# Softmax over a pair of PSUM banks: one maximum and one exponential for 1024 keys in the second block's attention

## The chip, the cores and the metric

The kernel runs on one core of a Trainium2 chip. The metric is the device time of one execution in microseconds (us). Three runs of the kernel before gave 3281.88, 3284.83 and 3296.58 us; the median, 3284.83 us, is what the change is measured against.

A core has five engines with a queue each, which run in the order in which the program was written down for them: TensorE (PE in the profile; PEld are its weight loads), VectorE (DVE), ScalarE (ACT), GpSimd (POOL) and SyncE (SP, which issues the transfers here). Matrix products go to PSUM, which has eight banks of 512 float32 per partition. DVE and ACT read them there.

## The reference

Two transformer blocks over 1024 tokens of width 1024. The second one runs two mixers side by side on the same normalized input, a grouped-query attention and a gated delta rule in both directions, and mixes their outputs. What the change touches is the attention:

```python
def gqa_attention(q, k, v):
    ...
    def block(qi):
        ...
        pr = jax.nn.softmax(s, axis=-1).astype(v.dtype)
```

There are 8 heads of 128 channels and 2 key heads; the scores of one query run over all 1024 keys, are scaled by 1/sqrt(128), and their softmax weighs the values. All of it is in float32.

## The kernel before

A product that must be as exact as float32 is split: `split` (L285 to L292) makes of an operand a rounded high part on ACT (L288, or on DVE) and the remainder on DVE or POOL (L292), and `mm3` (L278) adds three products, high by high, high by low and low by high, at L281, L282 and L283. So each product of 512 columns is three matmuls.

PSUM is handed out by hand. Eight tiles of one bank each are made once, and at the start of each stage `banks` says which banks serve which kind of tile (a tag), in turn. A tag may have a list of banks that it takes once, ahead of the ones that it takes in turn; by it a stage can start in banks that the stage before has already left. The tables stand at the head of the file (`B_DELTA`, `B_ATT2`).

Two stages of the second block matter here. The delta rule runs head by head. `delta_front` prepares a head's chunks. `delta_back` (from L1530) then walks through the 8 chunks of 128 tokens in both directions side by side, with a state from chunk to chunk: for each chunk and direction the products L1560 and L1562, a multiplication on DVE (L1568), the product L1576, the new state on DVE (L1583), and the output's products L1590 and L1591 with two more operations on DVE. In front of it and once within it, `correct` (L1540) makes products at L1547 and a copy at L1549. Behind the chunks stands the output's norm (L1606 to L1615), which needs ACT, DVE and POOL in turn. In `B_DELTA` the tag `wt` is that of `correct`, `vs` that of the chunk products and `o` that of the output's.

`attention2` (L1618) follows the last head. It transposes the keys (L1633, four transposes to a bank) and splits them and the values, and then runs 64 tiles of 128 queries: the queries in two halves, 8 heads in each, 4 tiles in each head, so 16 units of 4 tiles. `scores` makes a tile's 128 by 1024 scores in two banks, three matmuls in each, takes a maximum of each half on DVE as soon as that half stands (L1668), joins them and scales (L1670), and runs an exponential with a running sum for each half on ACT (L1672). DVE adds the two sums and inverts (L1674, L1675), and POOL multiplies the row (L1676). On the first tile of a unit the unit's queries are loaded, transposed (L1654) and split. `values` transposes a finished row by 128 keys (L1687), four to a bank of tag `tr`, splits each four, and after a unit's fourth tile runs the 24 matmuls with the values into the bank of tag `pv`, and DVE multiplies by the gate (L1697). `scores` is written five tiles ahead of `values`. Once in the loop stands the load and split of the weights `w_br_att_2` that the next stage needs (L1707, L307, L288 and L292).

The order on each queue is not that of the text. A scheduler takes the whole program, with its data dependencies and the tiles' reuse, and lays each engine's instructions down by the order of writing and by when it expects them to be ready. So the attention's start is interleaved with the last head of the delta rule where banks and memory allow it, and a change of banks can move instructions on all queues.

## Time and profile before

| What | us |
|---|---|
| Median of three runs (3281.88 to 3296.58) | 3284.83 |
| The profiled execution: span from its first to its last instruction | 3279.6 |
| PE busy in that span | 2982.4 (91%) |
| DVE busy | 2276.4 (69%) |
| ACT busy | 1422.1 (43%) |
| POOL busy | 1338.1 (41%) |

The page gives the profiled execution by its span; its own time isn't listed, and the median of the runs is 5.2 us above the span. A busy share is a mean over a long program with many stages. Where the change is made is a stretch of some 280 us, and what is read there is which engine is idle, and what ended its idle time. The durations of matmuls overlap: the distance between two starts tells what one costs PE.

### The profile page before, as it was taken

The page shows a single profiled execution, that of the slowest core. Times are in us where ns is not written, and L with a number is a line of the kernel's source. Part 1 is how long each engine was busy: PE and PEld are TensorE (multiplying, and loading weights), DVE is VectorE, ACT ScalarE, POOL GpSimd, SP SyncE. Part 2 cuts the span into 40 slices and gives each one's busy share as a digit, 9 for nine tenths or more (in the row PEclk, how much of TensorE's full clock was granted, in tenths as well). Part 3 has the DMA queues.
Part 4 walks back from the last instruction along what each step waited for, and adds up shares of the span by engine and source line. Part 5 has one row for each costly group of instructions (what it writes and reads, how often), then busy time and mean ns, then how long its engine had stood idle before and what let it go on. Part 6 is the DMA issues. An engine that isn't in the chain of part 4 may idle for free.

```text
span 3279.6 us, 47090 instructions
## 1 busy us (share of the span) xinstructions
PE 2982.4 (91%) x15982; PEld 2419.7 (74%) x15982; DVE 2276.4 (69%) x5568; ACT 1422.1 (43%) x2929; POOL 1338.1 (41%) x1364
## 2 busy tenths in 40 slices
PE   6988878998988789998999999999998989999898
PEld 2866667787666567776777888888887878778776
DVE  6699977865899949687765766685677588722322
ACT  3466417712666258334233334235434376621322
POOL 3432445565324354566533334334334242333422
PEclk8998989999998899999999999999998999999999
DMA  6122253332121231333333324324333221254421
GB/s 187 42 67 69 65 174 109 99 112 72 43 91 52 73 102 52 98 97 107 96 118 94 92 89 116 102 91 122 114 97 113 56 97 49 81 183 139 169 81 65
DMA packets 280013, 317.76 MB, mean 97 GB/s; under 512 B 97600, under 2 KB 180928, under 8 KB 279772
## 3 DMA queue, kind: packets, MB, share of 16 engines
q1 hardware_dynamic: 279772, 314.75, 31.5%
q8 instruction: 126, 2.06, 0.3%
q14 instruction: 115, 0.94, 0.1%
HBM read 226.48 MB, written 88.19 MB: 96 GB/s over the span
## 4 chain that ended last, share of the span: by engine, by line
PE 33%; DVE 8%; DMA 5%; ACT 2%; issue 2%; POOL 1%; SPq 0%; POOLq 0%; ACTq 0%; DVEq 0%
PE bank L281 8%; PE bank L282 8%; PE bank L283 8%; DVE block L1461 1%; DVE mem_float L1459 1%; PE bank L1687 1%; DVE mem_float32r L292 1%; ACT mem_float32r L288 1%; DVE mem_float L1668 1%; POOL mem_float32r L292 1%; DMA mem_float<-in_w_in_dram 1%; DMA mem_float<-in_w_br_dn_dram 1%; PE bank L1560 1%; PE bank L1547 1%; PE bank L1591 1%
## 5 line engine op out<-in xcount | busy, mean ns | idle before, releaser
L281 PE MATMUL bank<-mem_float32r 128*128 128x512 f32 (+2 forms) x2500 | 1007.0, 406 | 129.1 <-ACT mem_float32r L288 53.9
L282 PE MATMUL bank<-mem_float32r 128*128 128x512 f32 (+2 forms) x2508 | 999.7, 399 | 20.3 <-POOL mem_float32r L292 19.9
L283 PE MATMUL bank<-mem_float32r 128*128 128x512 f32 (+2 forms) x2500 | 979.7, 397 | 20.2 <-DVE mem_float32r L292 11.7
L281 PEld LDWEIGHTS bank<-mem_float32r 128*128 128x128 f32 (+1 forms) x2500 | 485.4, 194 | 249.1 <-ACT mem_float32r L288 64.7
L282 PEld LDWEIGHTS bank<-mem_float32r 128*128 128x128 f32 (+1 forms) x2508 | 487.7, 194 | 119.9 <-POOL mem_float32r L292 32.0
L283 PEld LDWEIGHTS bank<-mem_float32r 128*128 128x128 f32 (+1 forms) x2500 | 483.6, 194 | 119.0 <-POOL mem_float32r L292 12.3
L292 POOL TENSOR_TENSOR mem_float32r<-mem_float,mem_float32r 128x512 fp32r<-128x512 f32 (+3 forms) x158 | 220.1, 1395 | 276.4 <-ACT mem_float32r L288 204.9
L292 DVE TENSOR_TENSOR mem_float32r<-bank,mem_float32r 128x512 fp32r<-128x512 f32 (+3 forms) x392 | 233.3, 616 | 139.2 <-ACT mem_float32r L288 137.9
L292 POOL TENSOR_TENSOR mem_float32r<-block,mem_float32r 128x512 fp32r<-128x512 f32 (+3 forms) x189 | 247.2, 1314 | 176.0 <-ACT mem_float32r L288 167.4
L288 ACT ACTIVATE mem_float32r<-bank 128x512 fp32r<-128x512 f32 (+3 forms) x392 | 199.2, 543 | 114.4 <-PE bank L1687 46.8
L288 ACT ACTIVATE mem_float32r<-mem_float 128x512 fp32r<-128x512 f32 (+4 forms) x153 | 93.5, 614 | 325.9 <-DMA mem_float<-in_w_in_dram 144.8
L740 DVE TENSOR_SCALAR_CACHE_REDUCE block<-mem_float 128x384 bf16<-128x384 int16 (+7 forms) x280 | 229.2, 819 | 6.6 <-ACT mem_float L723 3.7
L276 POOL TENSOR_TENSOR mem_float<-mem_float 128x1 f32<-128x1 f32 (+3 forms) x136 | 121.4, 898 | 213.5 <-DVE mem_float L274 183.6
L288 ACT ACTIVATE mem_float32r<-block 128x512 fp32r<-128x512 f32 (+3 forms) x199 | 114.9, 585 | 158.6 <-DMA block<-in_w_in_dram 111.7
L1676 POOL TENSOR_SCALAR mem_float<-mem_float 128x1024 f32<-128x1024 f32 x64 | 72.8, 1137 | 156.8 <-DVE mem_float L1675 133.6
L281 PE MATMUL bank<-block,mem_float32r 128*128 128x512 f32 x300 | 119.9, 400 | 6.5 <-ACT mem_float32r L288 6.5
L283 PE MATMUL bank<-block,mem_float32r 128*128 128x512 f32 x300 | 118.1, 395 | 0.0
L1459 DVE TENSOR_TENSOR mem_float<-block,block 64x31 f32<-64x31 f32 (+15 forms) x248 | 94.8, 382 | 33.1 <-DMA block<-ud 27.1
L282 PE MATMUL bank<-block,mem_float32r 128*128 128x512 f32 x292 | 115.4, 395 | 0.0
L1219 DVE SCALAR_TENSOR_TENSOR mem_float<-mem_float 128x512 f32<-128x512 f32 x128 | 108.9, 869 | 0.3
L1461 DVE TENSOR_TENSOR block<-block,mem_float 64x31 f32<-64x31 f32 (+15 forms) x248 | 98.6, 398 | 6.1
L1672 ACT ACTIVATE mem_float<-bank,mem_float 128x512 f32<-128x512 f32 x128 | 86.9, 685 | 24.0 <-DVE mem_float L1675 14.0
(530 smaller groups left out, 6159.5 us busy)
## 6 DMA issues: line engine op xcount, KB each, us to landing
block<-in_w_in_dram SPq DMA_DIRECT2D x124, 256.0 KB, 2.7
block<-in_w_ada_dram SPq DMA_DIRECT2D x42, 512.0 KB, 4.4
mem_float<-in_w_in_dram SPq DMA_DIRECT2D x60, 256.0 KB, 2.8
mem_float<-in_w_out_dram SPq DMA_DIRECT2D x32, 256.0 KB, 2.6
x<-mem_float SPq DMA_DIRECT2D x16, 512.0 KB, 2.9
mem_float<-x SPq DMA_DIRECT2D x16, 512.0 KB, 3.2
block<-row_d SPq DMA_DIRECT2D x16, 512.0 KB, 4.1
qkv_d<-mem_float SPq DMA_DIRECT2D x32, 256.0 KB, 2.4
```

What stands on the lines that cost most here:

```text
L276: nc.gpsimd.tensor_tensor(out, out, self.mhalf[:, :n], op=OP.pow)
L281: mm(ps, ah, bh, start=start, stop=False)
L282: mm(ps, ah, bl, start=False, stop=False)
L283: mm(ps, al, bh, start=False, stop=stop)
L288: nc.scalar.activation(hi, src, AF.Copy)
L292: e.tensor_tensor(lo, src, f32(hi), op=OP.subtract)
L740: nc.vector.tensor_scalar(junk[:, :n], flat(key, blocks[j]), thr[:, j:j + 1], None, op0=op, op1=OP.add, accum_out=cnt[:, j:j + 1])
L1219: nc.vector.scalar_tensor_tensor(a, raw[:, r0 + j:r0 + j + 512], cw[:, ci, j:j + 1], a, op0=OP.mult, op1=OP.add)
L1459: nc.vector.tensor_tensor(t3, un[:, 0:b, b:b + 1].to_broadcast([64, b, n]), R[:, b:b + 1, b:32].to_broadcast([64, b, n]), op=OP.mult)
L1461: nc.vector.tensor_tensor(R[:, 0:b, b:32], R[:, 0:b, b:32], t3, op=OP.subtract)
L1672: nc.scalar.activation(p[:, c * 512:c * 512 + 512], ss[c], AF.Exp, scale=S2, bias=mx[:, 2:3], accum_out=mx[:, 3 + c:4 + c])
L1676: nc.gpsimd.tensor_scalar(p, p, mx[:, 5:6], 1.0, op0=OP.mult, op1=OP.mult)
```

## The change

A pair of PSUM banks can now be one tile of 1024 columns. The lower four banks stay single. The upper four belong to a region that is given up and taken again when the attention starts, as two pairs, and once more when the last stage starts, as four single banks. A query tile's scores go to one pair. One maximum over 1024 columns takes the place of two over 512 and the joining of them, one exponential the place of two, and the addition of the two sums goes. Per query tile that is 128 to 64 maxima and 128 to 64 exponentials in all, and 64 additions fewer. The number and size of the matmuls is the same.

The banks of the delta rule and of the attention are distributed anew. The delta rule's chunk products and outputs (`vs`, `wt`, `o`), which had banks 4 to 7, have banks 0 to 3, and its other tags the upper four. The attention's transposes begin in bank 2 (the delta rule's `wt`), then take 2, 0 and 1 in turn; `pv` is bank 3. Its first five score tiles all take the lower pair (banks 4 and 5), and those behind them the two pairs in turn. Before, the first five score tiles took banks 1 and 2, and the transposes began in banks 0 and 3.

The small tile `mx` has four columns in place of six and lies elsewhere in memory. Line numbers of the changed kernel are larger by up to 10: the maximum is L1678, its scaling L1679, the exponential L1680, the inversion L1681, POOL's product L1682; the transposes of the keys are L1644, of the queries L1665 and of the rows L1693.

```diff
-B_DELTA = dict(acc=("", (0, 1)), tr=("", (2, 3)), vs=("", (4, 5)), wt=("", (6,)), o=("", (7,)))
-B_ATT2 = dict(s=([1, 2] * 5, (1, 2, 3, 4)), tr=([0, 3] * 3, (0, 5, 6)), pv=("", (7,)))
+B_DELTA = dict(acc=("", (4, 5)), tr=("", (6, 7)), vs=("", (0, 1)), wt=("", (2,)), o=("", (3,)))
+B_ATT2 = dict(s=([4] * 5, (4, 5)), tr=([2] * 3, (2, 0, 1)), pv=("", (3,)))
...
-        self.bank = [ps.tile([P, 512], F32, name=f"bank{j}") for j in range(8)]
+        self.bank = [ps.tile([P, 512], F32, name=f"bank{j}") for j in range(4)]
+        self.upper = None
+        self.upper_banks("bank", 512)
...
+    def upper_banks(self, name, n):
+
+        if self.upper:
+            self.upper.close()
+        self.upper = self.ctx.enter_context(ExitStack())
+        ps = self.upper.enter_context(self.tc.tile_pool(name=self.uid("ps"), bufs=1, space=PSUM))
+        self.bank[4:] = [ps.tile([P, n], F32, name=self.uid(name)) for _ in range(2048 // n)]
...
         self.y_d = self.dram.tile([P, 8, S], F32, name="y2_d")
+        self.upper_banks("pair", 1024)
         self.banks(**B_ATT2)
...
-                mx = ap.tile([P, 6], F32, tag="mx2", bufs=8, name=self.uid("mx2"))
-                ss = []
+                mx = ap.tile([P, 4], F32, tag="mx2", bufs=8, name=self.uid("mx2"))
+                s = self.psum("s", (P, S))
                 for c in range(2):
-                    s = self.psum("s")
                     sl = slice(c * 512, c * 512 + 512)
-                    self.mm3(s, qT[0][:, t, :], qT[1][:, t, :], kT[0][:, g, sl], kT[1][:, g, sl], True, True)
-                    nc.vector.tensor_reduce(mx[:, c:c + 1], s, axis=AX.X, op=OP.max)
-                    ss.append(s)
-                nc.vector.tensor_scalar(mx[:, 2:3], mx[:, 0:1], mx[:, 1:2], -S2, op0=OP.max, op1=OP.mult)
-                for c in range(2):
-                    nc.scalar.activation(p[:, c * 512:c * 512 + 512], ss[c], AF.Exp, scale=S2, bias=mx[:, 2:3],
-                                         accum_out=mx[:, 3 + c:4 + c])
-                nc.vector.tensor_tensor(mx[:, 5:6], mx[:, 3:4], mx[:, 4:5], op=OP.add)
-                nc.vector.reciprocal(mx[:, 5:6], mx[:, 5:6])
-                nc.gpsimd.tensor_scalar(p, p, mx[:, 5:6], 1.0, op0=OP.mult, op1=OP.mult)
+                    self.mm3(s[:, sl], qT[0][:, t, :], qT[1][:, t, :], kT[0][:, g, sl], kT[1][:, g, sl], True, True)
+                nc.vector.tensor_reduce(mx[:, 0:1], s, axis=AX.X, op=OP.max)
+                nc.vector.tensor_scalar(mx[:, 1:2], mx[:, 0:1], -S2, None, op0=OP.mult)
+                nc.scalar.activation(p, s, AF.Exp, scale=S2, bias=mx[:, 1:2], accum_out=mx[:, 2:3])
+                nc.vector.reciprocal(mx[:, 3:4], mx[:, 2:3])
+                nc.gpsimd.tensor_scalar(p, p, mx[:, 3:4], 1.0, op0=OP.mult, op1=OP.mult)
                 return p
...
         wB = self.whole_w(pb, "w_br_dn_2", "b")
+        self.upper_banks("bank", 512)
         self.banks(**B_FIN)
```

What moves is read from the order of the two programs. First PE where the attention begins. Before, with the last head's first chunk products (L1547, L1560) around them; `bank1` and `bank2` hold the first scores:

```order
L1547 MATMUL bank6_69<-mem_float32_59,block8_5_10637 128x128
L1560 MATMUL bank5_68<-block5_7_10636,block4_5_12052 128x128
L1633 MATMUL bank3_66<-mem_float32_59 128x128 x4
L281 MATMUL bank1_64<-mem_float32r_58 128x512
L282 MATMUL bank1_64<-mem_float32r_58 128x512
L281 MATMUL bank2_65<-mem_float32r_58 128x512
L282 MATMUL bank2_65<-mem_float32r_58 128x512
L1576 MATMUL bank4_67<-block8_5_10637,block7_1_94 128x128
L1591 MATMUL bank7_70<-block8_5_10637,block9_7_12098 128x128
L283 MATMUL bank1_64<-mem_float32r_58 128x512
L283 MATMUL bank2_65<-mem_float32r_58 128x512
L1576 MATMUL bank5_68<-block8_5_10637,mem_float32_59 128x128
```

In the changed kernel the first scores stand here, behind the products of the last chunk (L1570 and L1572 are the old L1560 and L1562, L1600 and L1601 the old L1590 and L1591; `pair_3271` are banks 4 and 5):

```order
L1665 MATMUL bank0_63<-mem_float32_59 128x128 x4
L1570 MATMUL bank1_64<-block5_7_10639,block4_5_12055 128x128
L1572 MATMUL bank1_64<-block7_1_97,block8_5_10640 128x128
L1600 MATMUL bank3_66<-block7_1_97,block4_5_12055 128x128
L1601 MATMUL bank3_66<-block8_5_10640,block9_7_12101 128x128
L291 MATMUL pair_3271_19911<-mem_float32r_58 128x512
L292 MATMUL pair_3271_19911<-mem_float32r_58 128x512
L1665 MATMUL bank1_64<-mem_float32_59 128x128 x4
L293 MATMUL pair_3271_19911<-mem_float32r_58 128x512
L291 MATMUL pair_3271_19911<-mem_float32r_58 128x512
L292 MATMUL pair_3271_19911<-mem_float32r_58 128x512
```

The first scores moved from between the first and second chunk of the last head to behind its last chunk. Of the four groups of key transposes two stood ahead of that head's chunks and two in its first ones; now (L1644) all four stand between its fifth chunk and its seventh.

Second DVE where the last head's output norm ends. Before (L1609 to L1613 are the norm, L1668 a maximum, L1697 the first gate product):

```order
L1668 TENSOR_REDUCE mem_float32_59<-bank2_65 128x1
L1609 TENSOR_TENSOR mem_float32_59<-mem_float32_59 128x8
L1670 TENSOR_SCALAR mem_float32_59<-mem_float32_59 128x1
L1610 TENSOR_TENSOR mem_float32_59<-mem_float32_59 128x8
L274 TENSOR_SCALAR mem_float32_59<-mem_float32_59 128x8
L1674 TENSOR_TENSOR mem_float32_59<-mem_float32_59 128x1
L1675 RECIPROCAL mem_float32_59<-mem_float32_59 128x1
L292 TENSOR_TENSOR mem_float32r_58<-bank0_63,mem_float32r_58 128x4x128
L292 TENSOR_TENSOR mem_float32r_58<-bank6_69,mem_float32r_58 128x4x128
L1612 TENSOR_TENSOR mem_float32_59<-mem_float32_59 128x8
L1613 TENSOR_TENSOR block9_7_12098<-block9_7_12098,mem_float32_59 128x1024
L1697 TENSOR_TENSOR mem_float32_59<-bank7_70,mem_float32_59 128x512
```

In the changed kernel, between the maximum of the third tile to be scored (L1678) and that of the fourth, both in the lower pair; L1619 to L1623 are the norm:

```order
L1678 TENSOR_REDUCE mem_float32_59<-pair_3271_19911 128x1
L1679 TENSOR_SCALAR mem_float32_59<-mem_float32_59 128x1
L1619 TENSOR_TENSOR mem_float32_59<-mem_float32_59 128x8
L1620 TENSOR_TENSOR mem_float32_59<-mem_float32_59 128x8
L284 TENSOR_SCALAR mem_float32_59<-mem_float32_59 128x8
L1681 RECIPROCAL mem_float32_59<-mem_float32_59 128x1
L1622 TENSOR_TENSOR mem_float32_59<-mem_float32_59 128x8
L1623 TENSOR_TENSOR block9_7_12101<-block9_7_12101,mem_float32_59 128x1024
L1678 TENSOR_REDUCE mem_float32_59<-pair_3271_19911 128x1
L1679 TENSOR_SCALAR mem_float32_59<-mem_float32_59 128x1
```

The norm moved from behind the 24th half maximum, that is the twelfth tile, to between the third and the fourth tile.

Third ACT in one unit of the steady part. Before, behind two exponentials of a tile come the splits (L288) of three groups of row transposes, of the query transposes (`128x512`) and of two more groups, and then the next exponentials:

```order
L1672 ACTIVATE mem_float32_59<-bank3_66,mem_float32_59 128x512
L1672 ACTIVATE mem_float32_59<-bank4_67,mem_float32_59 128x512
L288 ACTIVATE mem_float32r_58<-bank0_63 128x4x128
L288 ACTIVATE mem_float32r_58<-bank6_69 128x4x128
L288 ACTIVATE mem_float32r_58<-bank5_68 128x4x128
L288 ACTIVATE mem_float32r_58<-bank0_63 128x512
L288 ACTIVATE mem_float32r_58<-bank6_69 128x4x128
L288 ACTIVATE mem_float32r_58<-bank5_68 128x4x128
L1672 ACTIVATE mem_float32_59<-bank1_64,mem_float32_59 128x512
```

In the changed kernel an exponential (L1680) stands ahead of the split of the group before the queries' (`bank1`) and of the queries' split (L298, `128x512`):

```order
L298 ACTIVATE mem_float32r_58<-bank2_65 128x4x128
L298 ACTIVATE mem_float32r_58<-bank0_63 128x4x128
L1680 ACTIVATE mem_float32_59<-pair_3272_19912,mem_float32_59 128x1024
L298 ACTIVATE mem_float32r_58<-bank1_64 128x4x128
L298 ACTIVATE mem_float32r_58<-bank2_65 128x512
L298 ACTIVATE mem_float32r_58<-bank0_63 128x4x128
L298 ACTIVATE mem_float32r_58<-bank1_64 128x4x128
```

The splits of a unit's row transposes, which stood together, now have whole exponentials between them.

## Rows read from the trace of the kernel before

**Rows 1.** The page, its head: span and number of instructions

```profile
span 3279.6 us, 47090 instructions
```

**Rows 2.** Busy time by stretch (us from the span's start), columns in its first line

```profile
core 0: us, PE busy (x) PEld busy (x) DVE busy (x) ACT busy (x) POOL busy (x), PEclk, DMA share, GB/s
2584.00:2611.00 27.00, 25.68 (x189) 23.43 (x188) 19.89 (x61) 19.93 (x48) 6.67 (x12) 1.00 0.13 40
2611.00:2640.00 29.00, 27.72 (x161) 22.73 (x160) 26.12 (x77) 18.14 (x57) 11.01 (x10) 1.00 0.09 29
2640.00:2660.00 20.00, 13.97 (x64) 10.79 (x63) 15.48 (x29) 10.51 (x24) 10.47 (x9) 0.83 0.39 118
2660.00:2690.00 30.00, 27.81 (x153) 22.47 (x151) 27.50 (x56) 23.39 (x52) 11.97 (x11) 1.00 0.42 140
2690.00:2846.00 156.00, 152.19 (x840) 126.81 (x840) 129.39 (x302) 105.84 (x252) 45.22 (x41) 1.00 0.14 48
2846.00:2860.00 14.00, 11.74 (x62) 9.40 (x63) 10.12 (x23) 9.46 (x22) 7.91 (x6) 1.00 0.51 164
```

**Rows 3.** Groups by line, 2690 to 2846: count, busy, mean ns, idle before

```profile
L281 PE MATMUL bank<-mem_float32r 128*128 128x512 f32 x160 | 67.9, 424 | 0.0
...
L292 DVE TENSOR_TENSOR mem_float32r<-bank,mem_float32r 128x512 fp32r<-128x512 f32 x91 | 60.1, 679 | 0.6
L1672 ACT ACTIVATE mem_float<-bank,mem_float 128x512 f32<-128x512 f32 x81 | 55.0, 684 | 19.2 <-DVE mem_float L1675 14.0 <-DVE mem_float L1674 5.3
L1668 DVE TENSOR_REDUCE mem_float<-bank 128x1 f32<-128x512 f32 x81 | 54.5, 683 | 5.6 <-PE bank L283 4.4
L288 ACT ACTIVATE mem_float32r<-bank 128x512 fp32r<-128x512 f32 x90 | 49.4, 600 | 31.3 <-PE bank L1687 19.7 <-PE bank L1654 11.5
...
L1687 PE MATMUL bank<-mem_float 128*128 128x128 f32 x320 | 45.3, 274 | 3.8 <-DVE mem_float32r L292 3.8
...
L1672 ACT ACTIVATION_READ_ACCUMULATOR mem_float<-bank,mem_float 128x1 f32 x80 | 15.7, 196 | 0.0
```

**Rows 4.** Timeline from 2701 us: start, duration, engine, line, operation, tiles, count

```profile
2701.01 0.20 DVE L1670 TENSOR_SCALAR mem_float<-mem_float 128x1 f32<-128x1 f32 x1
...
2702.33 1.27 DVE L1668 TENSOR_REDUCE mem_float<-bank 128x1 f32<-128x512 f32 x2
...
2703.46 0.60 PE L1687 MATMUL bank<-mem_float 128*128 128x128 f32 x4
...
2708.54 0.39 PE L283 MATMUL bank<-mem_float32r 128*128 128x512 f32 x1
...
2708.77 0.39 PE L281 MATMUL bank<-mem_float32r 128*128 128x512 f32 x1
```

**Rows 5.** Timeline of PE from 2584 us

```profile
2586.94 0.48 PE L281 MATMUL bank<-mem_float32r 128*128 128x512 f32 x1
...
2590.18 0.39 PE L1560 MATMUL bank<-block,mem_float 128*128 128x128 f32 x2
```

**Rows 6.** Timeline of PE, the delta loop of the head before

```profile
2505.51 0.49 PE L1560 MATMUL bank<-block,mem_float 128*128 128x128 f32 x2
...
2510.31 0.46 PE L1560 MATMUL bank<-block,block 128*128 128x128 f32 x2
```

**Rows 7.** Groups of ACT, 2584 to 2690

```profile
L1672 ACT ACT_TABLE_LOAD x1 | 1.3, 1283 | 0.0
```

**Rows 8.** Timeline of POOL and DVE from 2638 us

```profile
2638.50 1.66 POOL L276 TENSOR_TENSOR mem_float<-mem_float 128x8 f32<-128x8 f32 x1 [0.57 <-DVE mem_float L1674]
...
2641.33 2.27 DVE L1613 TENSOR_TENSOR block<-block,mem_float 128x1024 f32<-128x1024 f32 x1
```

**Rows 9.** Timeline of PE from 2653 us

```profile
2653.12 0.79 PE L281 MATMUL bank<-mem_float32r 128*128 128x512 f32 x1 [2.67 <-ACT mem_float32r L288]
...
2655.00 0.63 PE L282 MATMUL bank<-mem_float32r 128*128 128x512 f32 x1
2655.42 0.63 PE L283 MATMUL bank<-mem_float32r 128*128 128x512 f32 x1
```

2 rows, old and new, of the table PLACE are left out of this document.

## The prediction

> **What bounds the kernel now.** I read the page's head first: the profiled execution spans 3279.6 us [rows 1], 5.2 us less than the median of the runs, 3284.83. I take those 5.2 us as what lies around the span, unchanged, and add my sum to the median. Then I read the busy time by stretch, from the attention's first matmuls to its last [rows 2]. PE is the engine to look at. From 2690 to 2846, the steady part, it is busy 152.2 of 156 us at the full granted clock, DVE 129.4 and ACT 105.8. In the 56 us from 2584 to 2640, where the attention's start is interleaved with the delta rule's last head, PE is busy 25.7 of 27 and 27.7 of 29 us. It has its hole behind that, 14.0 of 20 us from 2640 to 2660, with a mean granted clock of 0.83, and then 27.8 of 30. So the attention is bound by PE nearly everywhere, and what the change saves on DVE and ACT counts only where PE waits for them.
>
> How much that is: the groups by line give 160 matmuls at L281 in the steady part, 16 to a unit of four query tiles, so 10 units in 156 us, 15.6 us a unit [rows 3]. What PE needs for one is counted from starts: matmuls of 512 columns follow each other every 0.23 us (more closely 0.227; 2708.54 and 2708.77), and four transposes take 0.60 us where the last alone takes 0.27, so 0.11 each [rows 3, 4]. A unit has 48 of the one and 36 of the other: 10.9 + 4.0 = 14.9 us. PE loses 0.7 us a unit to waits, and that is all a faster softmax can give back there.
>
> **The change part by part.** *The softmax itself.* Two maxima back to back take 1.27 us, one 0.68 [rows 3, 4]. One over 1024 columns lies between: not under 0.68, not over 1.27. I take 1.2, near the upper end, since the second of two costs 0.59 and nearly all of that is columns. Two exponentials and their sums (0.68 and 0.20) take 1.36 + 0.2 = 1.56 us; one lies between 0.88 and 1.56, and I take 1.3. The addition on DVE and a second operand of the scaling go, at most 0.2 us each by the 0.20 of the scaling. So DVE has about 0.3 us less per tile and ACT 0.25, but the maximum starts only after all six score matmuls, where half of it lay beside the last three.
>
> *Steady part.* What ended PE's idle time before L1687 is a DVE split [rows 3]. In the changed order ACT runs the exponential of a tile ahead of the splits of the last row group and of the unit's queries (the third place in the order above), and the next score matmuls need those queries. From the end of that tile's scores: 0.2 us to DVE, the maximum 1.2, one split that stands between 0.6, the scaling 0.2, 0.1 to ACT, exponential and sum 1.3, two splits 1.2 [rows 3], 0.1 back: 4.9 us. PE has in that time six score matmuls (1.37) and, by the order, 22 transposes (18 of rows, four of queries, 2.4): 3.8 us. It waits about 1.1 us a unit where it waits 0.7 now. Eleven units stay steady: +0.4 x 11 = +4.4 us. The bounds are all of the wait gone, -0.7 x 11 = -7.7, and a wait longer by as much, +7.7.
>
> *The start: the largest term.* The order shows the first scores behind the last chunk of the last head, because the transposes and banks now come from the delta rule's own `wt`, `vs` and `o`, which that head uses to its end. Before, they start at 2586.94, and chunk 1 of that head at 2590.18 [rows 5]. Alone, a direction of a chunk takes 1.6 us: in the head before, where nothing is interleaved, four L1560 stand from 2505.51 to 2510.31, three steps in 4.80 us [rows 6]. Thirteen steps behind 2590.2 is 2611.0, so the first scores come at about 2611, 24 us late. PE isn't idle meanwhile. The head has 88 products of two passes of 0.11 us, 19.4 us, and 20 transposes of keys and queries, 2.2 us: 21.6 of the 27 us from 2584 on. It loses 5.4 where it loses 1.3 now [rows 2]: +4.1.
>
> Then the five first tiles must take the lower pair one after the other. Each needs its scores 1.4, the step to DVE 0.2, the maximum 1.2, scaling and steps 0.4, exponential and sum 1.3, together 4.5 us, and PE has beside it only 1.4 of scores and 0.9 of eight row transposes. Four such waits of 2.2 are 8.8 us. The first exponential loads its table, 1.3 us [rows 7]; before, chunk products fill that time. And the output norm now stands on DVE between the third tile's maximum and the fourth's: its operations include 1.66 us on POOL, which DVE waits for, and 2.27 on DVE [rows 8], about 4 us in the way of that tile. 8.8 + 1.3 + 4.0 = 14.1, less the 1.3 that the 29 us from 2611 lose now: +12.8. If PE finds other work in all of these waits this is 0, which the order speaks against: there is no projection left, and row products need finished rows.
>
> *The hole from 2640 to 2660* has two causes now, the same norm and weight splits for which ACT waits on transfers. The norm's part is paid above, so I take 2.5 of the 6.0 us off; nothing off or all of it are the bounds. Weights still follow the attention's start, and I leave their part as it is.
>
> *The clock.* After waits of PE up to 2.67 us in that hole, the matmuls from 2653 on stand 0.42 us apart (2655.00, 2655.42), the distance of the lower level, 1.2 GHz [rows 9]; the mean of 0.83 over those 20 us [rows 2] is about 7 us at that level. The start above has waits of the same size, one after the other. Two tiles' scores and transposes at half the clock cost 2 x 2.3 = 4.6 us, less about 2.5 that the hole costs now: +2. Bounds: none, and five such tiles, +9.
>
> *The end and the rest.* The last tile's maximum waits for all of its scores, +0.6. The delta rule's heads before the last are reordered a little on PE, with the same instructions; there PE is bound or not by the same things, and I take 0, between -5 and +5. The reused banks at the last stage cost nothing: its first products follow the attention's last exponentials anyway.
>
> Sum: 4.4 + 4.1 + 12.8 - 2.5 + 2 + 0.6 = +21.4 us, so 3306 us.
>
> **The Trainium skill.** The steady part shows DVE busy 129.4 of 156 us, ACT 105.8, PE 152.2 [rows 2]: neither of the two is full. The Trainium skill (Perfetto Trace Analysis, Optimizing Scalar/DVE Operations) says that grouping into larger operations can help throughput if the engine is saturated, and that where ACT and DVE are not saturated but cause bubbles elsewhere, breaking instructions up may let work finish sooner. By the first half the change gains, a rival below; by the second it loses, as in the sum; the trace fits the second in the steady part, while from 2660 to 2690, with DVE busy 27.5 of 30, it fits the first.
>
> **Rivals.** *Faster.* DVE is nearly full from 2611 to 2640 and from 2660 to 2690, 26.1 of 29 and 27.5 of 30 us [rows 2]. If it were the engine that sets the pace in these stretches and the pair were free in time, 0.3 us for each of some 20 tiles, 6 us, and the steady waits of 7.7 would go: -13.7, were the start not later; with half of the start's term, 8.5, it ends at -5, 3280 us. Against it: PE, not DVE, is busy 92 to 96% there. That is the Trainium skill's first half, worked out.
>
> *The late start is made good.* PE's work is the same, and a late start costs only idle PE. If rows and queries prepared meanwhile fill the waits, half the 14.1 goes, the hole from 2640 goes wholly (-6.0), the clock stays up: 4.4 + 4.1 + 5.8 - 6.0 + 0.6 = +9, 3294 us. For it: ACT and POOL are far from full. Against it: all first tiles share one pair.
>
> *The pair also stalls the steady part.* With two pairs, a tile's scores need the whole exponential of the tile before the last. If DVE runs late by one split, 0.7 us, in each of 11 units, +7.7 in place of +4.4, and the clock falls for five tiles (+9 in place of 2): +32, 3317 us. It decides where PE's wait before the first score matmul of a unit passes 1.5 us.
>
> *The change doesn't do what it says.* The maximum over two banks could cost two separate passes; it is then 1.27 and the steady wait 1.2. That moves 1 us.
>
> **How the numbers follow.** The sum's case has 0.66 of the chance, with +10 to +30 as its own range; made good 0.18, +2 to +12; the steady stall 0.12, +25 to +40; faster 0.04. Half a per cent, 16.4 us, is about what a measurement of this kernel can tell from no change. Of the sum's case two thirds lie over it, 0.44; with the stall, slower has 0.56. The rest of it and the case made good, 0.22 + 0.18, give 0.40 for no change. Faster by that much needs 3268, which no case reaches as it stands; I leave 0.04. The range takes the lower half of the good case off and most of the stall in: 3286 to 3323.
>
> **What would show it.** The first scores (L291 into a pair) at about 2611 us from the start, behind the last L1572; idle PE of 2 us and more before four score groups between 2611 and 2642, released by ACT's L1680, one of them 5 us or more with the norm (L1619 to L1623) on DVE inside it; a lower granted clock there; a steady unit of 16.0 us, and the attention's end about 20 us later. The prediction is wrong if the first scores come before 2600, if PE is over 85% busy from 2611 to 2642, or if a unit takes under 15.3 us.

## The result and the profile after

Six runs of the changed kernel have a median of 3315.23 us (3305.71 to 3320.68), six of the kernel before 3286.98: the ratio is 1.0076, with a 95% interval of 1.0061 to 1.0091, so +25 us. A second series, E10 below, gave 1.0106 (1.0083 to 1.0129). The change makes the kernel slower; 3306 us was forecast, 3286 to 3323 as the range.

The head of the page of the changed kernel, and its busy time by engine; it answers to [rows 1]:

```profile
span 3319.0 us, 46731 instructions
...
PE 2999.4 (90%) x15982; PEld 2427.1 (73%) x15982; DVE 2257.1 (68%) x5440; ACT 1408.8 (42%) x2803; POOL 1336.5 (40%) x1364
```

Its span is 39.4 us longer than that of [rows 1], more than the 28 us between the medians: the profiled run is the slowest of its six. DVE and ACT have less to do than before (there 2276.4 and 1422.1 us), and the kernel gained nothing by it. Where the time went is read from four stretches, cut at events that both kernels have: the first chunk product of the delta rule, the last group of products of the last `delta_front`, the query transposes of the attention's sixth unit, those of its last unit, and the end. Busy time by stretch in the changed kernel (columns in the first line):

```profile
core 0: us, PE busy (x) PEld busy (x) DVE busy (x) ACT busy (x) POOL busy (x), PEclk, DMA share, GB/s
1781.40:2598.80 817.40, 779.66 (x5321) 662.40 (x5320) 535.64 (x1442) 303.01 (x615) 287.00 (x361) 0.95 0.36 101
2598.80:2710.60 111.80, 94.01 (x547) 79.52 (x546) 76.91 (x166) 63.22 (x128) 38.32 (x37) 0.92 0.23 72
2710.60:2869.40 158.80, 155.23 (x842) 126.96 (x841) 117.35 (x221) 94.94 (x172) 45.05 (x40) 1.00 0.15 49
2869.40:3319.00 449.60, 418.21 (x1908) 339.75 (x1906) 130.92 (x187) 116.22 (x201) 146.30 (x103) 0.98 0.38 125
```

And the same four stretches of the kernel before, in a second profile of it (E9 below; in the profile of the rows above they took 799.5, 100.1, 156.7 and 440.1 us):

```profile
1776.40:2584.00 807.60, 779.63 (x5329) 665.09 (x5327) 532.41 (x1444) 300.91 (x614) 289.77 (x361) 0.95 0.36 102
2584.00:2684.60 100.60, 89.95 (x538) 75.17 (x538) 83.11 (x206) 67.39 (x168) 39.76 (x39) 0.97 0.23 74
2684.60:2841.20 156.60, 152.27 (x842) 126.78 (x841) 130.05 (x302) 105.92 (x252) 45.10 (x40) 1.00 0.15 52
2841.20:3287.40 446.20, 416.16 (x1905) 338.83 (x1903) 130.23 (x193) 116.00 (x207) 145.01 (x101) 0.98 0.39 127
```

With a second profile of the changed kernel too (E10), the means of two profiles each are: heads of the delta rule 803.6 and 816.4, attention's start 100.4 and 111.6, ten steady units 156.7 and 158.8, the rest 443.2 and 448.8. So +12.8, +11.2, +2.1 and +5.6, together +31.7; what lies ahead differs by 0.2. The sum forecast 0, +16.4, +4.0 and +1.0.

The attention's start, in three pieces, in the changed kernel; it answers to the first three stretches of [rows 2]:

```profile
2598.80:2624.30 25.50, 24.88 (x212) 23.36 (x211) 17.88 (x55) 11.76 (x27) 3.69 (x10) 1.00 0.06 21
2624.30:2656.50 32.20, 19.20 (x90) 14.61 (x88) 22.12 (x44) 18.52 (x42) 15.48 (x11) 0.89 0.28 83
2656.50:2710.60 54.10, 49.94 (x249) 41.54 (x250) 36.91 (x69) 32.94 (x60) 19.15 (x16) 0.91 0.29 90
```

In the first the last head runs alone, and PE is idle for 0.6 us. In the second, from the first scores on, PE loses 13.0 of 32.2 us. The clock is at 0.89 there and 0.91 behind it. PE's timeline shows what it waited for (start, duration, engine, line, operation, tiles, count, idle time before it and what ended it); it answers to [rows 5] and [rows 9]:

```profile
2624.32 0.48 PE L291 MATMUL pair<-mem_float32r 128*128 128x512 f32 x1
...
2630.90 0.50 PE L291 MATMUL pair<-mem_float32r 128*128 128x512 f32 x1 [2.68 <-ACT mem_float L1680]
...
2632.17 0.39 PE L293 MATMUL pair<-mem_float32r 128*128 128x512 f32 x1
...
2640.18 0.79 PE L291 MATMUL pair<-mem_float32r 128*128 128x512 f32 x1 [5.70 <-ACT mem_float L1680]
...
2641.20 0.63 PE L293 MATMUL pair<-mem_float32r 128*128 128x512 f32 x1
2641.63 0.63 PE L291 MATMUL pair<-mem_float32r 128*128 128x512 f32 x1
...
2646.24 0.58 PE L291 MATMUL pair<-mem_float32r 128*128 128x512 f32 x1 [2.19 <-ACT mem_float L1680]
...
2652.63 0.50 PE L291 MATMUL pair<-mem_float32r 128*128 128x512 f32 x1 [0.23 <-ACT mem_float L1680]
```

The four waits for the lower pair, each ended by ACT's exponential, are 2.68, 5.70, 2.19 and 0.23 us. Behind the longest the matmuls stand 0.43 us apart (2641.20, 2641.63), the distance of the 1.2 GHz level. DVE, ACT and POOL around the 5.70 us; the norm's rows answer to [rows 8], the table load to [rows 7]:

```profile
2628.35 1.28 ACT L1680 ACT_TABLE_LOAD   x1 [2.25 <-DVE mem_float L1679]
...
2636.37 1.21 DVE L1678 TENSOR_REDUCE mem_float<-pair 128x1 f32<-128x1024 f32 x1
...
2637.62 0.15 DVE L1679 TENSOR_SCALAR mem_float<-mem_float 128x1 f32<-128x1 f32 x1
2638.12 0.63 ACT L298 ACTIVATE block<-mem_float 128x512 fp32r<-128x512 f32 x1 [0.36 <-DMA mem_float<-in_w_br_att_dram]
...
2638.95 1.09 ACT L1680 ACTIVATE mem_float<-pair,mem_float 128x1024 f32<-128x1024 f32 x1
...
2639.79 1.65 POOL L286 TENSOR_TENSOR mem_float<-mem_float 128x8 f32<-128x8 f32 x1 [3.08 <-DVE mem_float L284]
...
2641.67 1.95 DVE L1623 TENSOR_TENSOR block<-block,mem_float 128x1024 f32<-128x1024 f32 x1
...
2643.55 1.21 DVE L1678 TENSOR_REDUCE mem_float<-pair 128x1 f32<-128x1024 f32 x1
```

The tile's scores were done at 2632.6. Its maximum starts 3.8 us later, behind the last chunk's outputs and the splits that stand ahead of it on DVE, and its exponential 1.2 us after the scaling, behind a weight split on ACT that waits for a transfer. The norm's power on POOL and its 1.95 us product on DVE come behind that tile, and delay only the next maximum, by some 0.4 us (it starts 1.07 us behind the start of its tile's last matmul, the maximum after it 0.67). The table load lies inside the first wait, of 2.68 us.

The steady part, groups by line (count, busy time, mean ns of one, idle time before them); it answers to [rows 3]:

```profile
L302 DVE TENSOR_TENSOR mem_float32r<-bank,mem_float32r 128x512 fp32r<-128x512 f32 x91 | 59.8, 680 | 9.2 <-ACT mem_float32r L298 9.2
...
L1678 DVE TENSOR_REDUCE mem_float<-pair 128x1 f32<-128x1024 f32 x40 | 48.7, 1219 | 11.2 <-PE pair L293 11.2
...
L1680 ACT ACTIVATE mem_float<-pair,mem_float 128x1024 f32<-128x1024 f32 x41 | 45.7, 1115 | 42.7 <-DVE mem_float L1679 42.7
...
L291 PE MATMUL pair<-mem_float32r 128*128 128x512 f32 x80 | 34.2, 427 | 3.6 <-ACT mem_float32r L298 3.6
...
L1680 ACT ACTIVATION_READ_ACCUMULATOR mem_float<-pair,mem_float 128x1 f32 x40 | 7.8, 194 | 0.0
```

One maximum over 1024 columns takes 1.22 us where two took 1.27, and one exponential 1.11 with 0.19 for its sum, where two took 1.36 with 0.40. The unit's length is read from the query transposes, by their first and last start:

```profile
L1665 PE MATMUL bank<-mem_float x48: 272/273/273, 2694.8 to 2869.8; 128*128 128x128 f32 x48
```

48 of them are 12 units; from the first of the first to the first of the last are 2869.8 - 0.3 - 2694.8 = 174.7 us, 15.88 a unit, against 15.6 before. In the ten units this gives +2.1 us and not +2.8, since the first of the ten takes 16.3 us in the kernel before. PE's idle time there isn't longer, 3.6 us where it was 4.3; the same 842 matmuls keep PE busy for 155.2 us in place of 152.3, at a granted clock of 1.00 in both, so they stand a little further apart. E8 finds a part of the reason.

### The profile page after: what moved, and what is told of

The parts are those of the page before. It is cut to its first block, busy times and chain, and to the rows that moved or that the text cites. A ratio compares the mean times of both kernels' runs of the same rounds, so it can differ in the third digit from the quotient of the medians.

```text
span 3319.0 us, 46731 instructions
## 1 busy us (share of the span) xinstructions
PE 2999.4 (90%) x15982; PEld 2427.1 (73%) x15982; DVE 2257.1 (68%) x5440; ACT 1408.8 (42%) x2803; POOL 1336.5 (40%) x1364
## 5 line engine op out<-in xcount | busy, mean ns | idle before, releaser
L291 PE MATMUL bank<-mem_float32r 128*128 128x512 f32 (+1 forms) x2372 | 949.1, 404 | 131.8 <-ACT mem_float32r L298 54.8
L292 PE MATMUL bank<-mem_float32r 128*128 128x512 f32 (+2 forms) x2380 | 953.5, 401 | 24.7 <-POOL mem_float32r L302 24.4
L293 PE MATMUL bank<-mem_float32r 128*128 128x512 f32 (+1 forms) x2372 | 934.9, 399 | 19.9 <-DVE mem_float32r L302 10.3
L291 PEld LDWEIGHTS bank<-mem_float32r 128*128 128x128 f32 x2372 | 461.3, 195 | 250.3 <-ACT mem_float32r L298 68.1
L292 PEld LDWEIGHTS bank<-mem_float32r 128*128 128x128 f32 (+1 forms) x2380 | 463.9, 195 | 124.7 <-POOL mem_float32r L302 39.3
L293 PEld LDWEIGHTS bank<-mem_float32r 128*128 128x128 f32 x2372 | 460.4, 195 | 111.7 <-POOL mem_float32r L302 14.1
L298 ACT ACTIVATE mem_float32r<-mem_float 128x512 fp32r<-128x512 f32 (+4 forms) x153 | 93.5, 614 | 346.3 <-DMA mem_float<-in_w_in_dram 131.7
L298 ACT ACTIVATE mem_float32r<-bank 128x512 fp32r<-128x512 f32 (+3 forms) x392 | 198.5, 542 | 98.0 <-PE bank L1693 36.1
L298 ACT ACTIVATE mem_float32r<-block 128x512 fp32r<-128x512 f32 (+3 forms) x199 | 115.1, 585 | 158.4 <-DMA block<-in_w_in_dram 111.3
L1682 POOL TENSOR_SCALAR mem_float<-mem_float 128x1024 f32<-128x1024 f32 x64 | 72.5, 1134 | 174.8 <-DVE mem_float L1681 163.9
L1680 ACT ACTIVATE mem_float<-pair,mem_float 128x1024 f32<-128x1024 f32 x64 | 71.3, 1114 | 58.7 <-DVE mem_float L1679 58.7
```

Source lines behind the costliest of these rows:

```text
L291: mm(ps, ah, bh, start=start, stop=False)
L292: mm(ps, ah, bl, start=False, stop=False)
L293: mm(ps, al, bh, start=False, stop=stop)
L298: nc.scalar.activation(hi, src, AF.Copy)
L1680: nc.scalar.activation(p, s, AF.Exp, scale=S2, bias=mx[:, 1:2], accum_out=mx[:, 2:3])
L1682: nc.gpsimd.tensor_scalar(p, p, mx[:, 3:4], 1.0, op0=OP.mult, op1=OP.mult)
```

## The experiments

Ratios are to the kernel before, run on the same chip. The stretches are those above, in us; tail is the last of them.

| Run | ratio (95% interval) | heads | start | ten units | tail |
|---|---|---|---|---|---|
| before, two profiles | 1 | 799.5, 807.6 | 100.1, 100.6 | 156.7, 156.6 | 440.1, 446.2 |
| changed, two profiles | 1.0076, 1.0106 | 817.4, 815.4 | 111.8, 111.3 | 158.8, 158.8 | 449.6, 448.0 |
| E1 bank numbers only | 1.0020 (1.0005 to 1.0034) | 814.3 | 99.7 | 156.6 | 440.7 |
| E2 order kept | 1.0046 (1.0028 to 1.0064) | 804.2 | 113.6 | 158.9 | 449.3 |
| E3 late, single banks | 1.0071 (1.0050 to 1.0092) | 812.5 | 103.7 | 159.0 | 451.8 |
| E4 pair, two halves | 1.0237 (1.0214 to 1.0260) | 817.9 | 121.8 | 181.9 | 461.5 |
| E5 E2, pairs in turn | 1.0042 (1.0026 to 1.0057) | 802.0 | 104.7 | 164.8 | 444.7 |
| E6 E2, early, one pair | 1.0049 (1.0032 to 1.0066) | 795.9 | 110.8 | 158.9 | 444.3 |
| E7 E2, early, in turn | 1.0034 (1.0021 to 1.0046) | 807.7 | 104.1 | 158.8 | 447.8 |
| E8 E2, queries earlier | 1.0061 (1.0044 to 1.0078) | 799.5 | 115.7 | 161.7 | 445.3 |
| E11 E7 and E8 | 1.0047 (1.0030 to 1.0064) | 802.9 | 107.7 | 161.8 | 449.1 |
| E12 E2, half maxima | 1.0147 (1.0128 to 1.0167) | 795.7 | 119.0 | 178.1 | 455.0 |

**E1, bank numbers only.** The kernel before, with

```diff
-B_DELTA = dict(acc=("", (0, 1)), tr=("", (2, 3)), vs=("", (4, 5)), wt=("", (6,)), o=("", (7,)))
-B_ATT2 = dict(s=([1, 2] * 5, (1, 2, 3, 4)), tr=([0, 3] * 3, (0, 5, 6)), pv=("", (7,)))
+B_DELTA = dict(acc=("", (4, 5)), tr=("", (6, 7)), vs=("", (0, 1)), wt=("", (2,)), o=("", (3,)))
+B_ATT2 = dict(s=([5, 6] * 5, (5, 6, 7, 0)), tr=([4, 7] * 3, (4, 1, 2)), pv=("", (3,)))
```

> The kernel before, with only the bank numbers of the delta rule and of the second attention exchanged (lower four for upper four), single banks, two maxima and two exponentials, attention started early as before. On PE its delta heads stand in exactly the order of the changed kernel. Theory A (the profile of the changed kernel is right about the heads: they take 16 to 18 us longer because the delta rule now takes over other banks from the stage before it, which reorders 1437 of 8822 instructions on PE): +8 to +18 us against the kernel before. Theory B (my prediction's term: the reordering costs nothing, and those 16 us are this one execution's): within 6 us of the kernel before.

**E2, order kept.** The changed kernel, with the five tables ahead of `B_DELTA` exchanged too, one of them shown:

```diff
-B_IN2 = dict(acc=("", (0, 1, 2)), s=("", (3, 4, 5)), tr=("", (6, 7)))
+B_IN2 = dict(acc=("", (4, 5, 6)), s=("", (7, 0, 1)), tr=("", (2, 3)))
```

> The changed kernel, with the bank numbers of the stages ahead of the delta rule exchanged as well, so that the delta heads stand on PE in exactly the order of the kernel before; pairs, late start, one maximum and one exponential stay. Theory A (the reordered heads are over half of the loss): +8 to +15 us against the kernel before. Theory B (the loss is the late start and the serial first tiles): +20 to +28 us, as the changed kernel (+25).

Heads of E1, busy time (columns as above), and heads and start of E2:

```profile
1790.80:2605.10 814.30, 779.58 (x5329) 661.10 (x5327) 536.32 (x1444) 302.20 (x616) 286.16 (x361) 0.95 0.36 101
```

```profile
1780.10:2584.30 804.20, 776.42 (x5323) 663.50 (x5323) 531.24 (x1441) 300.97 (x613) 292.18 (x361) 0.95 0.36 102
2584.30:2697.90 113.60, 95.06 (x546) 80.14 (x544) 76.35 (x166) 63.69 (x128) 37.74 (x37) 0.91 0.23 71
```

The heads of E1 take 814.3 us, those of E2 804.2. Of all profiles, nine in the old order have 795.7 to 807.7 us, mean 801.7, with 26.2 to 30.4 us of idle PE; five in the new one 812.5 to 817.9, mean 815.5, with 34.7 to 39.2. The two sets don't overlap. So the reordered heads cost 13.8 us by these means, 8.5 of it idle PE; the rest is PE's own busy time, higher by 5 (a mean clock of 0.95 in four of those five, of 0.95 or 0.96 in the nine). The times agree in direction and are less sure of the size. E1 is at about +7 us, between theory B's 6 and theory A's 8, and 2 to 11 by its interval, so that its times alone decide for neither; its profiled run is the second slowest of twelve. E2 is at +15, at the upper end of theory A's 8 to 15 and below theory B's 20. But "over half of the loss", as theory A has it there, isn't borne out: the heads are 12.8 of 31.7 us.

**E3, late start with single banks.** The kernel before, with the changed `B_DELTA` and

```diff
+B_ATT2 = dict(s=([4, 5] * 5, (4, 5, 6, 7)), tr=([2] * 3, (2, 0, 1)), pv=("", (3,)))
```

> The kernel before with the changed kernel's banks for the delta rule and the attention, but four single banks for the scores and two maxima and two exponentials of 512 columns: the transposes wait for the delta rule's own banks as in the changed kernel, so the first scores come behind the last chunk of the last head. Theory B (late start and serial first tiles, whatever the width of the softmax): +15 to +24 us, a unit of four tiles at 15.6 us. Rival C (the loss comes from holding a pair and from the wide maximum): within 6 us of the run with only the bank numbers exchanged.

The time came as theory B said, +23 us, but not from where it said: heads +8.9 and tail +8.6 make most of it, and the start only +3.3 against the kernel before. So a late start with single banks costs 3 to 4 us there. The unit is 15.6 to 15.7 us, as expected; two of the ten take 17.6 and 16.2, which makes the 159.0.

**E4, a pair, but halves.** The changed kernel with the maximum and the exponential in the loop over the halves again:

```diff
-                nc.vector.tensor_reduce(mx[:, 0:1], s, axis=AX.X, op=OP.max)
+                    nc.vector.tensor_reduce(mx[:, c:c + 1], s[:, sl], axis=AX.X, op=OP.max)
...
-                nc.scalar.activation(p, s, AF.Exp, scale=S2, bias=mx[:, 1:2], accum_out=mx[:, 2:3])
+                    nc.scalar.activation(p[:, sl], s[:, sl], AF.Exp, scale=S2, bias=mx[:, 2:3],
+                                         accum_out=mx[:, 3 + c:4 + c])
```

> The changed kernel with its pairs, but two maxima and two exponentials of 512 columns on the halves of the pair: only the merging is undone. By my sum the chain from a tile's last scores to the free pair is 0.2 to 0.5 us shorter at the maximum (half of it lies beside the last three score matmuls) and 0.25 longer at the exponential, so the time is within 5 us of the changed kernel's +25. Rival (the Trainium skill's larger operations gain here, hidden under the late start): 6 us or more slower than the changed kernel, +31 or more. Rival C (the wide operations are the loss): +15 or less.

My sum missed: +78 us, a unit at 17.7 to 19.3, which is beyond the rival's +31 too. Once a pair is held, the merged operations are worth 2.3 us a unit. E12 shows why.

**E5 to E7, the start repaired.** E5 is E2 with `s=("", (4, 5))`. E6 is E2 with the first six groups of transposes in halves of the upper pair; E7 is both, with five such groups:

```diff
+        self.bank += [self.bank[5][:, :512], self.bank[5][:, 512:]]
-B_ATT2 = dict(s=([4] * 5, (4, 5)), tr=([2] * 3, (2, 0, 1)), pv=("", (3,)))
+B_ATT2 = dict(s=("", (4, 5)), tr=([6, 7, 6, 7, 6], (2, 0, 1)), pv=("", (3,)))
```

> The kernel of the run with the order kept (changed kernel, delta heads in the order of before), but the first score tiles take the two pairs in turn instead of the lower one five times; the start stays late. Theory (the serial first pair is its own term): PE's waits for ACT's exponential in the first five tiles, 10.8 us together in the changed kernel, fall to 4 to 6, so 4 to 7 us less than the run with the order kept, about 3299. Rival (the wait only moves, to the rows, the norm and the splits behind): within 2 us of it, 3303 to 3307.

> The run with the order kept, but the first six groups of transposes (keys and queries) go to the two halves of the upper pair, which is free before the last head's chunks end, instead of the delta rule's own bank; the first five score tiles still take the lower pair. By the order the first scores then stand behind the 9th of the last head's 16 chunk products and not behind its last. Theory (the late start is the larger term, up to 16 us): 6 to 12 us less than the run with the order kept, 3293 to 3299. Rival (the serial pair is the larger term and stretches the start wherever it lies): at most 3 us less.

> Both repairs at once: transposes of the keys and of the first queries in the halves of the upper pair, and the first score tiles in the two pairs in turn. If late start and serial pair are the whole loss of the attention's start, 12 to 16 us less than the run with the order kept: 3289 to 3294, the kernel before within 5 us, with the steady unit still at 15.9 us (+3). Rival (a pair as such costs PE at the start): 3298 or more.

The stretch of the start in E5, in E6 and in E7:

```profile
2580.00:2684.70 104.70, 89.83 (x545) 74.70 (x543) 77.48 (x169) 63.96 (x130) 37.74 (x38) 0.98 0.24 78
```

```profile
2580.70:2691.50 110.80, 95.14 (x545) 79.42 (x542) 76.65 (x166) 63.23 (x128) 38.44 (x37) 0.90 0.23 73
```

```profile
2584.00:2688.10 104.10, 89.05 (x546) 74.84 (x545) 76.19 (x166) 62.98 (x128) 38.39 (x37) 0.98 0.25 78
```

Against E2's 113.6 us, the pairs in turn take 8.9 off the start, the early transposes 2.8, both 9.5. So the serial first pair is the larger term, and E6's rival was right. In E5 PE's waits for ACT's exponential in the start are 5.3 us, for 11.7 in E2, as expected. E6 and E7 have the first scores 10 us earlier, of the some 22 by which they are late; those 10 us are worth 3 beside the serial pair and under 1 without it. The clock tells the same: 0.90 in E6 and 0.91 in E2, where PE waits for the one pair, 0.98 in E5 and E7. In the whole time it shows little: E5 is 1 us below E2, which is what its rival said, since it loses 5.9 us again in the units, which are at 16.4 us there. E7 is the best of the pair versions, but at +11 us not within the 5 us that were expected. No version here beats the kernel before.

**E8, queries one tile earlier.** `queries` holds the lines that load, transpose and split; the loop calls it one tile ahead:

```diff
                 if i + ahead < 64:
                     ps.append(scores(i + ahead))
+                queries(i + ahead + 1)
```

> The run with the order kept, with each unit's queries loaded, transposed and split one tile earlier in the order of writing. Theory (in the steady part PE waits for the query split, which ACT has behind a tile's exponential): the unit of four tiles falls from 15.9 to 15.6 us or less, 3 to 5 us less in all. Rival (the 0.3 us are the maximum that waits for a whole tile, not the queries): the unit stays at 15.9.

The unit fell to 15.7 us, nearly as the theory said, but only behind four units of 17.5 to 22.3, two of them in the ten: 161.7 us for the ten. So 0.2 of the 0.3 us a unit goes with the place of the queries, and moving them buys nothing in all.

**E9 and E10, both kernels once more.** E9 is a single execution, 3289.13 us.

> The kernel before once more, for a second profile. Theory D (the last stage behind the attention isn't touched by the change; the 388 us that it took in the profile of before, against 395 to 403 in the changed kernel and the eight experiments, was a short one of several): 394 to 398 us from the last gate product of the attention to the end. Rival E (every variant with the exchanged banks or the pairs costs the last stage 7 to 10 us): 388 again, within 2 us.

> The changed kernel once more, for a second profile and on the same chip as the other runs of this group. Theory (attention's start and steady part are fixed by the order): the waits for the first pair again 2.2 to 2.7 us, 5.7 us and 2.2 us, the unit 15.9 us, and 16 us within 3 from the first scores behind the heads to the end of the attention more than before; the delta heads 7 to 18 us longer than before. Time +20 to +29 us.

From the end of the last gate product to the end of the span lie 391.2 us in the first profile (388 by the expectation's count) and 394.9 in E9: 3.7 more, between the 6 to 10 of theory D and the 2 of rival E. In the changed kernel it is 400.8 and 402.0. So some of the first difference of 10 was that profile's, and the means of two still differ by 8, or by 5.6 over the tail of the table, which begins earlier. In the first 40 us of the tail PE is busy 37.5 and 37.4 us before, 35.9 and 35.7 after. The rest is spread over the waits for the last stage's weights, which vary by as much between two profiles of one kernel; it stays open. E10 repeats the four waits, the third one shorter (2.69, 5.50, 1.63 and 0.16 us), the unit of 15.9 and, within 2 us, heads and start; its time, +35 us, is above the 20 to 29 expected.

**E11, both.** E7 with E8's edit.

> The run with transposes in the upper pair and both pairs in turn, and each unit's queries one tile earlier as well. If both repairs add, attention's start is 4 to 5 us longer than in the kernel before and the unit 15.7 us in place of 15.9: 2 us less than the former, +6 to +10 us against the kernel before. Rival (earlier queries cost the start what they save later, as the run with them alone shows, with two units of 17.5 to 18.5 us before the steady ones): +12 or more.

The rival was right, +15 us: the slow units come with the earlier queries here too.

**E12, half maxima, one exponential.** E2 with the maxima of E4 and the exponential of the changed kernel.

> The run with the order kept, with two maxima of 512 columns, each as soon as its half stands, and one exponential over 1024. Theory (the steady 0.3 us are the maximum that starts only behind all six score matmuls): the unit falls to 15.6 to 15.7 us, and each of the first four waits for the pair by 0.5 us, so 4 to 6 us less than the run with the order kept, about +10. Rival (two halves cost more on DVE and in the order than they save, as with two maxima and two exponentials): a unit over 16.5 us and +25 or more.

The theory fell, +48 us, and the rival held. PE's order shows what the half maxima change (`pair_3271` and `pair_3272` are the two pairs; the first of each three score matmuls stands for a half tile). In E12:

```
L291 MATMUL pair_3271_19911<-mem_float32r_58 128x512
L291 MATMUL pair_3272_19912<-mem_float32r_58 128x512
...
L291 MATMUL pair_3271_19911<-mem_float32r_58 128x512
L291 MATMUL pair_3272_19912<-mem_float32r_58 128x512
```

and in the changed kernel:

```
L291 MATMUL pair_3271_19911<-mem_float32r_58 128x512
L291 MATMUL pair_3271_19911<-mem_float32r_58 128x512
...
L291 MATMUL pair_3272_19912<-mem_float32r_58 128x512
L291 MATMUL pair_3272_19912<-mem_float32r_58 128x512
```

With a maximum for each half the scheduler runs two tiles abreast, a half of the one and a half of the other (E4 has the same order). So both pairs are full late and together. What ended PE's waits in E12 from 2733 to 2850 us (in total, times, longest), and one such wait with DVE and ACT ahead of it:

```profile
PE pair L291 <- ACT mem_float L1680: 14.2, 7, 2.0
```

```profile
2783.41 1.37 DVE L1678 TENSOR_REDUCE mem_float<-pair 128x1 f32<-128x512 f32 x2
...
2786.36 0.68 DVE L1678 TENSOR_REDUCE mem_float<-pair 128x1 f32<-128x512 f32 x1
...
2787.56 0.68 DVE L1678 TENSOR_REDUCE mem_float<-pair 128x1 f32<-128x512 f32 x1
...
2788.40 1.11 ACT L1680 ACTIVATE mem_float<-pair,mem_float 128x1024 f32<-128x1024 f32 x1
...
2789.65 0.50 PE L291 MATMUL pair<-mem_float32r 128*128 128x512 f32 x1 [2.02 <-ACT mem_float L1680]
2789.77 1.12 ACT L1680 ACTIVATE mem_float<-pair,mem_float 128x1024 f32<-128x1024 f32 x1 [0.17 <-DVE mem_float L1679]
```

The first two halves of two tiles have their maxima at 2783.41, the second halves at 2786.36 and 2787.56; the exponentials follow each other at 2788.40 and 2789.77, and PE, which has no free pair, stands for 2.02 us until the first is done. One maximum over the whole tile keeps a tile's scores together: it is the order that the merged operation brings, more than its duration, that is worth 2 us a unit in a pair. The seven waits make 2.2 us of a unit's 17.8; halves in the old order were not tried, so this rests on the trace. With single banks (the kernel before) each half is a buffer of its own, and this doesn't arise.

The Trainium skill (Perfetto Trace Analysis, Optimizing Scalar/DVE Operations) says that breaking up instructions may let work finish sooner where ACT and DVE aren't saturated but leave others idle. The prediction took the steady part for such a place. In single banks the runs agree: broken up, the unit is 15.6 us (the kernel before, E3), merged in a pair 15.9. E4 and E12 don't agree: in both the softmax broken up in a pair makes the unit 1.6 to 3.4 us longer than the merged one.

## Why the prediction came out, and where it didn't

The direction and the size were right, and partly by luck, because two errors cancel: the heads had nothing and cost 12.8 us, and the start had 16.4 and cost 11.2. With the heads' order kept, which the sum takes for granted, E2 measures +15 us and not +21.

- **"I take 0, between -5 and +5"** for the heads ahead of the last is the step that failed: +12.8. I looked at the instructions, which are the same, and not at the banks that `B_DELTA` takes over from the stage before it. E1 has only those numbers changed and has the loss; E2 has the pairs and doesn't. Which waits make it is spread over many lines, and why PE's busy time rises with it stays open.
- **The head alone, +4.1.** PE loses 0.6 us of 25.5, where I counted 5.4 of 27: alone the head is nearly all PE work. The first scores come 25.5 us behind the last front product, 27 were forecast; they are at 2624 and not 2611 only because the heads were late, and in E2 they are at 2611.4. So this loss isn't where I put it; a late start costs 3 to 4 us in all with single banks (E3), and with pairs in turn 10 us less of it are worth 0.6 (E7 against E5).
- **The five first tiles, +12.8**, is the right mechanism: 13.0 us of idle PE in that stretch, 10.8 of it in four waits for the lower pair, and E5 gets 8.9 of the start back. Its parts were priced wrongly: 2.2 us for each of four waits and 4.0 for the norm. A wait of over 5 us came as forecast, but by another cause: it is made by the last chunk's outputs and a weight split ahead of the tile, and the norm lies behind. The fourth wait is 0.2, since transposes and a tile in the upper pair (from 2650.55) fill it.
- **The clock, +2.** The mean over the start is 0.92 and 0.94, against 0.97 before, and PE's busy time there is 4.0 and 2.7 us longer.
- **The hole, -2.5.** Behind 2656.5 PE loses 4.2 of 54.1 us, where it lost 8.2 of 50 from 2640 to 2690 [rows 2]. So some 4 us came off, as far as the two stretches can be set side by side.
- **The steady part, +4.4 for eleven units**, 16.0 us each: 15.88 measured, +0.28 a unit, 0.2 of it with the place of the queries (E8). The size came out, the wait only in part: before the score matmuls PE is idle for 0.36 us a unit, ended by an ACT split, where I counted 1.1; the wait for the row splits, 0.38 a unit before [rows 3], is gone for it. The rest of the growth is no idle time. The maximum was taken at 1.2 and is 1.22. The exponential with its sum was taken at 1.3, and is 1.11 and 0.19.
- **The end, +0.6**: the tail has +5.6, as far as two profiles each can tell.
- **The 5.2 us around the span** are mostly the spread of the runs: every run listed with its span lies 1.6 to 2.2 us above it. The sum starts from the median, so nothing in it moves.

Of the rivals, "faster" needed DVE to set the pace; DVE is busy 117 of 159 us in the ten units, where it was 130 of 157, and PE is bound as before. "Made good" holds for most of the lateness and not for the serial pair. "The pair also stalls the steady part" isn't so with one maximum and one exponential, but is with halves.

## What to carry to other kernels

Taking over banks in another order is itself a change, in every stage that touches the ones handed over: where a scheduler lays down the queues, compare its order there too, and exchange the numbers alone to price it. Before merging two operations over two buffers, ask who waits for the buffers: a merged buffer is free only when its last reader is done, so the first tiles must not share one (8.9 us of the start here, of which 1 was left in the whole time). And a smaller operation isn't only shorter: it lets a scheduler start the next tile in between, which is wrong where two tiles then hold all the buffers.

## What the runs showed of the hardware

One maximum over 1024 float32 columns in two PSUM banks took 1.22 us and two back to back over 512 took 1.27: 0.05 us for the instruction saved. On ACT an exponential of 1024 columns took 1.11 us, two of 512 start 0.68 apart (E4), so 0.25 saved.
